# Order of the matmul passes within one weight tile: all with the high part first, then all with the low part

## The chip, the cores and the metric

The kernel runs on one core of a Trainium2 chip. The metric is the device time of one execution in microseconds (us). Before the change the median of three timed runs is 1946.19 us (1943.83 to 1947.27). One further execution was profiled; it took 1940.68 us.

## The reference, cut to what matters

One layer of a network on 256 tokens of width 2048: a mixer (gated delta rule, gated linear attention and a state-space part, merged by gates), cross attention to 256 memory tokens, and a convolved feed-forward block of hidden width 5632. All weights are float32. What matters for this change is that nearly all of the work is plain products of the 256 tokens with weight matrices:

```python
z = h @ w_in                          # 2048 x 14368, split into q, k, v, gates, ...
y_a = o_a @ w_dn_out                  # and w_gla_out, w_s5_glu, w_mix_out
q = h @ w_xa_q; kv = mem_n @ w_xa_kv  # and w_xa_out
gate, up = jnp.split(h @ w_ffn_up, 2, axis=-1)
y = (jax.nn.gelu(causal_depthwise_conv(gate, ffn_conv_w)) * up) @ w_ffn_down
```

## The kernel before

**Split numbers.** Each float32 operand is written as a high part in the type fp32r plus a low part (the remainder, also fp32r). A product is then three passes on TensorE: weight high by input high, weight high by input low, weight low by input high.

**Weight tiles.** Weights come in tiles of 2 blocks of 128 rows (KG = 2, the index kk) by 512 columns. `load_w` makes one: SyncE starts the DMA into `raw` (4 buffers), ScalarE casts it to `whi` (3 buffers, line 206, named CAST in the profile), and VectorE subtracts to get `wlo` (3 buffers, also line 206, TENSOR_TENSOR). A new `whi` can be cast when TensorE has read the oldest one for the last time; the same holds for `wlo`.

**Two forms of product.** `proj` gives a result with features on partitions: a weight block of 128x128 is the stationary operand, and the input moves. Its high pass (line 218; line 221 at the end of the contraction) streams 512 columns, which are the input's high and low halves side by side, and its low pass (line 219) streams 256. A tile has 4 output blocks m, so 8 high and 8 low passes. Before the change they alternate: for each m, for each kk, high then low. `proj_tok` gives tokens on partitions: 128 tokens of the input are stationary and 512 weight columns move. For each of two token halves t and each kk it makes the passes of lines 285 (weight high, input high), 286 (weight high, input low) and 287 (weight low, input high). `proj2` is `proj` over two weights at once, for the start of the feed-forward block. Results gather in PSUM tiles `acc`, of which there are five; those of `proj` are emptied by `total` (lines 225 and 226) and what follows it (in the delta-rule part `conv_silu`, lines 387 to 393).

**Order.** The engines run their own instructions in the order that the program lists, each waiting for what it needs. That order is fixed when the program is built: a scheduler that simulates a timeline picks from what is ready, with weight loads at a raised priority. So code order is only a start: it lets the scheduler move work of the background parts (the state-space recurrence of lines 932 to 934, the delta rule, the norms) and of the evacuations between the passes, and it also moves passes. A change in the passes can therefore move instructions of VectorE and ScalarE too, though the diff has none.

Of the kernel before, what the change touches and what calls it, by code (L numbers as in the profile page):

```python
# [9 lines left out]
F32 = mybir.dt.float32  # L10
# [8 lines left out]
P = 128  # L19
T = 256  # L20
# [3 lines left out]
NW = 512  # L24
KG = 2
# [11 lines left out]
N_ACC = 5  # L37
# [51 lines left out]
class Net:  # L89
# [116 lines left out]
            self.last = (nc.scalar.copy(hi, raw), self.seq(lambda: nc.vector.tensor_sub(lo, raw, hi.bitcast(F32))))  # L206
        return hi, lo

    def mm3(self, acc, hi, lo, x, start, stop):
        nc = self.nc  # L210
        if acc.shape[1] == T:
            nc.tensor.matmul(acc, hi, x[:, 0, :], start=start, stop=False)
            nc.tensor.matmul(acc, hi, x[:, 1, :], start=False, stop=False)
            nc.tensor.matmul(acc, lo, x[:, 0, :], start=False, stop=stop)
            return
        both = x.rearrange("p c s -> p (c s)")
        if not stop:
            nc.tensor.matmul(acc, hi, both, start=start, stop=False)  # L218
        nc.tensor.matmul(acc[:, :T], lo, x[:, 0, :], start=False, stop=False)  # L219
        if stop:  # L220
            nc.tensor.matmul(acc, hi, both, start=start, stop=True)  # L221

    def total(self, acc, out=None):
        r = self.row() if out is None else out
        self.nc.scalar.copy(r, acc[:, T:2 * T])  # L225
        self.nc.vector.tensor_add(r, r, acc[:, 0:T])  # L226
        return r

    def proj(self, w, KT, rhs, evac, n=NW, wide=True):
        nc = self.nc  # L230
        nm = (n + P - 1) // P
        accs = []
        for m in range(nm):
            a = self.ps_acc.tile([P, 512], F32, name="acc", tag="acc")
            accs.append(a[:min(P, n - m * P), :2 * T if wide else T])
        G = KT // KG
        for g in range(G):
            hi, lo = self.load_w(w, g, n)
            for m in range(nm):
                ms = slice(m * P, min(n, (m + 1) * P))  # L240
                for kk in range(KG):
                    kt = g * KG + kk
                    self.mm3(accs[m], hi[:, kk, ms], lo[:, kk, ms], rhs(kt), kt == 0, kt == KT - 1)
            if g < G - 1:
                self.pump()
        for m in range(nm):
            evac(m, accs[m])
        self.pump()

    def proj2(self, ws, KT, rhs, evac):  # L250
        nc = self.nc
        accs = []
        for i in range(6):
            a = self.ps_acc.tile([P, 512], F32, name="acc", tag="acc") if i < N_ACC else self.mx([P, 512])
            accs.append(a)
        for g in range(KT // KG):
            for i, w in enumerate(ws):
                nm = 4 - 2 * i
                hi, lo = self.load_w(w, g, nm * P)
                for m in range(nm):  # L260
                    ms = slice(m * P, (m + 1) * P)
                    for kk in range(KG):
                        kt = g * KG + kk
                        self.mm3(accs[4 * i + m], hi[:, kk, ms], lo[:, kk, ms], rhs(kt), kt == 0, kt == KT - 1)
                self.pump()
        for i in range(6):
            evac(i, accs[i])

    def proj_tok(self, w, KT, lhs, evac, n=NW, tail=1, mid=None):
        nc = self.nc  # L270
        accs = [self.ps_acc.tile([P, 512], F32, name="acc", tag="acc")[:, :n] for _ in range(2)]
        G = KT // KG
        wts = {}
        last = []

        def part(t, g):
            if g not in wts:
                wts[g] = self.load_w(w, g, n)
            hi, lo = wts[g]
            ts_ = slice(t * P, (t + 1) * P)  # L280
            for kk in range(KG):
                kt = g * KG + kk
                x = lhs(kt)
                xh, xl = (x[0], x[1]) if isinstance(x, tuple) else (x[:, 0, :], x[:, 1, :])
                nc.tensor.matmul(accs[t], xh[:, ts_], hi[:, kk, :], start=(kt == 0), stop=False)  # L285
                nc.tensor.matmul(accs[t], xl[:, ts_], hi[:, kk, :], start=False, stop=False)  # L286
                last[:] = [nc.tensor.matmul(accs[t], xh[:, ts_], lo[:, kk, :], start=False, stop=(kt == KT - 1))]  # L287

        for g in range(G - tail):
            for t in range(2):  # L290
                part(t, g)
            if mid and g == (G - tail) // 2:
                mid()
            self.pump()
        for t in range(2):
            with self.after(last if t and tail > 1 else ()):
                for g in range(G - tail, G):
                    part(t, g)
            evac(t, accs[t])
        self.pump()  # L300

# [1272 lines left out]
```

## Time and profile before

| what | value |
|---|---|
| median of three timed runs | 1946.19 us |
| profiled execution, time | 1940.68 us |
| profiled execution, span from first to last instruction | 1938.9 us |
| ScalarE (ACT) busy | 951.8 us, 49% |
| mean share of the 16 DMA engines, main queue | 54.9% |
| read from HBM | 350.47 MB, 187 GB/s over the span |

The profile names TensorE PE (its weight loads PEld), VectorE DVE, ScalarE ACT, GpSimd POOL and SyncE SP. A matmul's row gives its start and its duration, but matmuls are pipelined: the next one starts before the last has ended. So what a matmul costs is read from start to start, which is called its step here. In rows that merge several, the duration is from the first start to the last end.

### The profile page before, as it was taken

Reading aid. Unit: us, or ns where it says so; the run is one execution under the profiler, and the core shown is the slowest. Engines: PE = TensorE matmul, PEld = TensorE weight load, DVE = VectorE, ACT = ScalarE, POOL = GpSimd, SP = SyncE. Lnnn points to the kernel's source line nnn. Section 1 sums busy time; section 2 is a strip of 40 time slices with the busy share of each in tenths; the row PEclk is TensorE's granted clock in tenths of the full one; section 3 lists DMA queues with packets and bytes.
Section 4 is the critical chain, followed back from the end, with each engine's and each line's share of the span. In section 5 each row is a group of like instructions: output and inputs, shape, how many; then the busy total and the mean of one; then the engine's idle time right before and its main releaser. Section 6 shows DMA issues by size and latency. Waiting matters only on the chain.

```text
span 1938.9 us, 28177 instructions
## 1 busy us (share of the span) xinstructions
PE 1878.7 (97%) x10440; PEld 1565.4 (81%) x10440; DVE 1419.8 (73%) x2719; ACT 951.8 (49%) x1426; POOL 67.4 (3%) x117
## 2 busy tenths in 40 slices
PE   7989899999999999999999997999999999999997
PEld 6778788777778688878877986888888888888886
DVE  6878999996579999967666756766666666644445
ACT  5655544343565444444455655555555555534442
POOL 0000012020000000000000000000000000000000
PEclk9999999999999999999999998999999999999999
DMA  7535477684445576666576544655666555676664
GB/s 254 174 109 172 152 206 233 191 254 131 131 121 172 184 219 179 213 218 203 186 264 210 173 155 144 213 184 174 190 195 189 187 185 185 206 224 200 200 192 135
DMA packets 107482, 363.93 MB, mean 188 GB/s; under 512 B 12320, under 2 KB 20896, under 8 KB 106832
## 3 DMA queue, kind: packets, MB, share of 16 engines
q1 hardware_dynamic: 97696, 328.32, 54.9%
q0 software_dynamic: 9648, 33.81, 5.3%
q8 instruction: 82, 1.34, 0.3%
q14 instruction: 56, 0.46, 0.1%
HBM read 350.47 MB, written 11.61 MB: 187 GB/s over the span
## 4 chain that ended last, share of the span: by engine, by line
PE 86%; DVE 6%; issue 4%; DMA 2%; ACT 1%; POOL 0%; SPq 0%; DVEq 0%; ACTq 0%; POOLq 0%
PE acc L218 25%; PE acc L219 14%; PE acc L287 13%; PE acc L285 13%; PE acc L286 13%; DVE wlo L206 2%; PE acc L221 2%; PE mx L922 2%; DMA raw<-in 1%; DVE f L519 1%; DVE mm L932 0%; PE mx L183 0%; PE mx L947 0%; PE mx L641 0%; ACT whi L206 0%
## 5 line engine op out<-in xcount | busy, mean ns | idle before, releaser
L206 DVE TENSOR_TENSOR wlo<-raw,whi 128x1024 fp32r<-128x1024 f32 (+1 forms) x632 | 753.0, 1195 | 417.2 <-ACT whi L206 415.1
L206 ACT CAST whi<-raw 128x1024 fp32r<-128x1024 f32 (+1 forms) x632 | 646.7, 1029 | 724.8 <-PE acc L286 376.0
L218 PE MATMUL acc<-aa,whi 128*128 128x512 f32 x2085 | 725.8, 401 | 11.5 <-DVE r L226 9.7
L219 PE MATMUL acc<-aa,wlo 128*128 128x256 f32 x2224 | 555.2, 284 | 9.9 <-DVE wlo L206 9.9
L219 PEld LDWEIGHTS acc<-aa,wlo 128*128 128x128 f32 x2224 | 421.9, 190 | 53.3 <-DVE wlo L206 20.9
L218 PEld LDWEIGHTS acc<-aa,whi 128*128 128x128 f32 x2085 | 386.1, 190 | 82.2 <-issue 11.7
L285 PE MATMUL acc<-whi,aa 128*128 128x512 f32 (+1 forms) x704 | 269.8, 384 | 0.0
L286 PE MATMUL acc<-whi,aa 128*128 128x512 f32 (+1 forms) x704 | 268.4, 382 | 0.0
L287 PE MATMUL acc<-wlo,aa 128*128 128x512 f32 (+1 forms) x704 | 253.3, 385 | 3.7 <-DVE wlo L206 3.7
L287 PEld LDWEIGHTS acc<-wlo,aa 128*128 128x128 f32 x704 | 131.9, 188 | 33.6 <-DVE wlo L206 7.3
L286 PEld LDWEIGHTS acc<-whi,aa 128*128 128x128 f32 x704 | 132.4, 188 | 26.4 <-issue 1.1
L285 PEld LDWEIGHTS acc<-whi,aa 128*128 128x128 f32 x704 | 132.3, 188 | 26.2 <-issue 1.2
L285 PE MATMUL acc<-whi,ach 128*128 128x512 f32 x352 | 136.9, 389 | 0.0
L286 PE MATMUL acc<-whi,acl 128*128 128x512 f32 x352 | 136.9, 389 | 0.0
L287 PE MATMUL acc<-wlo,ach 128*128 128x512 f32 x352 | 123.4, 389 | 0.0
L932 DVE TENSOR_TENSOR mm<-M,X 128x128 f32<-128x128 f32 x254 | 98.6, 388 | 5.3 <-ACT X L926 0.6
L286 PEld LDWEIGHTS acc<-whi,acl 128*128 128x128 f32 x352 | 66.0, 188 | 13.8
L287 PEld LDWEIGHTS acc<-wlo,ach 128*128 128x128 f32 x352 | 66.1, 188 | 13.7
L285 PEld LDWEIGHTS acc<-whi,ach 128*128 128x128 f32 x352 | 66.1, 188 | 13.7
L934 DVE TENSOR_TENSOR X<-X,s__868 128x64 f32<-128x64 f32 x255 | 71.5, 280 | 4.5
L933 DVE TENSOR_TENSOR s__868<-mm 128x64 f32<-128x64 f32 x255 | 56.5, 222 | 4.7
L226 DVE TENSOR_TENSOR r<-r,acc 128x256 f32<-128x256 f32 x143 | 57.1, 414 | 0.4 <-ACT r L225 0.3
(454 smaller groups left out, 1865.6 us busy)
## 6 DMA issues: line engine op xcount, KB each, us to landing
raw<-in SPq DMA_DIRECT2D x600, 512.0 KB, 4.1
raw<-in SPq DMA_DIRECT2D x32, 256.0 KB, 2.7
gd<-r POOLq DMA_DIRECT2D x24, 256.0 KB, 4.7
f<-gd POOLq DMA_DIRECT2D x12, 512.0 KB, 5.3
f<-Rd POOLq DMA_DIRECT2D x4, 512.0 KB, 7.0
f<-in POOLq DMA_DIRECT2D x4, 512.0 KB, 4.0
gp<-in POOLq DMA_DIRECT2D x8, 256.0 KB, 4.5
xn<-in POOLq DMA_DIRECT2D x1, 2048.0 KB, 11.1
```

The source lines that it names most:

```text
L206: self.last = (nc.scalar.copy(hi, raw), self.seq(lambda: nc.vector.tensor_sub(lo, raw, hi.bitcast(F32))))
L218: nc.tensor.matmul(acc, hi, both, start=start, stop=False)
L219: nc.tensor.matmul(acc[:, :T], lo, x[:, 0, :], start=False, stop=False)
L221: nc.tensor.matmul(acc, hi, both, start=start, stop=True)
L226: self.nc.vector.tensor_add(r, r, acc[:, 0:T])
L285: nc.tensor.matmul(accs[t], xh[:, ts_], hi[:, kk, :], start=(kt == 0), stop=False)
L286: nc.tensor.matmul(accs[t], xl[:, ts_], hi[:, kk, :], start=False, stop=False)
L287: last[:] = [nc.tensor.matmul(accs[t], xh[:, ts_], lo[:, kk, :], start=False, stop=(kt == KT - 1))]
L922: nc.tensor.matmul(ps[:, n, c, :], self.Bl[c][rs, ft, :], su[rs, ft, tk], start=True, stop=True, tile_position=(32 * q, 0))
L932: nc.vector.tensor_mul(m, self.M, prev[:, None].broadcast_to([P, 2, 2, 32]))
L933: nc.vector.tensor_add(s, m[:, :, 0, :], m[:, :, 1, :])
L934: nc.vector.tensor_add(X[:, :, :, t], X[:, :, :, t], s)
```

## The change

Within one weight tile, `proj`, `proj2` and `proj_tok` now write all passes with `whi` first and all passes with `wlo` after them. In the last tile of a contraction, `proj` keeps the passes of one output block together (high, low, low, high), as before. The number, the shapes and the operands of the passes stay the same; so do the loads and all other code. A branch for 256-wide accumulators that nothing called is dropped.

```diff
-    def mm3(self, acc, hi, lo, x, start, stop):
-        nc = self.nc
...
-        both = x.rearrange("p c s -> p (c s)")
-        if not stop:
-            nc.tensor.matmul(acc, hi, both, start=start, stop=False)
-        nc.tensor.matmul(acc[:, :T], lo, x[:, 0, :], start=False, stop=False)
-        if stop:
-            nc.tensor.matmul(acc, hi, both, start=start, stop=True)
...
+    def tile_passes(self, accs, hi, lo, rhs, g, KT, n):
+        nc = self.nc
+        ks = [g * KG + kk for kk in range(KG)]
+        xs = [rhs(k) for k in ks]
+        ms = [slice(m * P, min(n, (m + 1) * P)) for m in range(len(accs))]
+
+        def high(m, kk):
+            nc.tensor.matmul(accs[m], hi[:, kk, ms[m]], xs[kk].rearrange("p c s -> p (c s)"), start=ks[kk] == 0,
+                             stop=ks[kk] == KT - 1)
+
+        def low(m, kk):
+            nc.tensor.matmul(accs[m][:, :T], lo[:, kk, ms[m]], xs[kk][:, 0, :], start=False, stop=False)
+
+        if ks[-1] < KT - 1:
+            for f in (high, low):
+                for m in range(len(accs)):
+                    for kk in range(KG):
+                        f(m, kk)
+            return
+        for m in range(len(accs)):
+            for kk in range(KG - 1):
+                high(m, kk)
+            for kk in range(KG):
+                low(m, kk)
+            high(m, KG - 1)
...
     def proj2(self, ws, KT, rhs, evac):
...
                 hi, lo = self.load_w(w, g, nm * P)
-                for m in range(nm):
-                    ms = slice(m * P, (m + 1) * P)
-                    for kk in range(KG):
-                        kt = g * KG + kk
-                        self.mm3(accs[4 * i + m], hi[:, kk, ms], lo[:, kk, ms], rhs(kt), kt == 0, kt == KT - 1)
+                self.tile_passes(accs[4 * i:4 * i + nm], hi, lo, rhs, g, KT, nm * P)
                 self.pump()
...
-        def part(t, g):
+        def passes(ts, g):
             if g not in wts:
                 wts[g] = self.load_w(w, g, n)
             hi, lo = wts[g]
-            ts_ = slice(t * P, (t + 1) * P)
-            for kk in range(KG):
-                kt = g * KG + kk
...
-                nc.tensor.matmul(accs[t], xh[:, ts_], hi[:, kk, :], start=(kt == 0), stop=False)
-                nc.tensor.matmul(accs[t], xl[:, ts_], hi[:, kk, :], start=False, stop=False)
-                last[:] = [nc.tensor.matmul(accs[t], xh[:, ts_], lo[:, kk, :], start=False, stop=(kt == KT - 1))]
...
+            for t in ts:
+                for kk in range(KG):
+                    for i in range(2):
+                        nc.tensor.matmul(accs[t], xs[kk][i][:, t * P:(t + 1) * P], hi[:, kk, :],
+                                         start=ks[kk] == 0 and i == 0, stop=False)
+            for t in ts:
+                for kk in range(KG):
+                    last[:] = [nc.tensor.matmul(accs[t], xs[kk][0][:, t * P:(t + 1) * P], lo[:, kk, :], start=False,
+                                                stop=ks[kk] == KT - 1)]
 
         for g in range(G - tail):
-            for t in range(2):
-                part(t, g)
+            passes(range(2), g)
```

In the changed kernel line 222 is the high pass of `proj` and line 226 its low pass, line 282 the two high passes of `proj_tok` and line 286 its low pass; `total` has moved to lines 211 and 212, and the lines behind `proj_tok` have moved up by one.

What the built programs list shows what the scheduler made of it. **First place: TensorE, the first weight tiles of the program** (`xset` is the split input, `acc` the accumulators). Before:

```order
L218 MATMUL acc<-xset,whi 128x512
L219 MATMUL acc<-xset,wlo 128x256
L218 MATMUL acc<-xset,whi 128x512
L219 MATMUL acc<-xset,wlo 128x256
L218 MATMUL acc<-xset,whi 128x512
L219 MATMUL acc<-xset,wlo 128x256
```

The same place in the changed program:

```order
L222 MATMUL acc<-xset,whi 128x512 x8
L226 MATMUL acc<-xset,wlo 128x256 x8
L222 MATMUL acc<-xset,whi 128x512 x8
L226 MATMUL acc<-xset,wlo 128x256 x8
L222 MATMUL acc<-xset,whi 128x512 x8
```

High and low passes have moved apart into runs of eight. At other places the scheduler keeps runs of two, where accumulators come free one by one. Counted over the whole list of TensorE, a low pass of `proj` follows directly on a high pass 1886 times before and 597 times now.

**Second place: VectorE, the end of the first slab of delta-rule keys** (`r1` and `f16` belong to `conv_silu` of the accumulators 840 and 841; `zs` is a copy for the state-space part; 1158 and 1180 are weight tiles of the next slab). Before:

```order
L206 TENSOR_TENSOR wlo_1158<-raw_1156,whi_1157 128x1024
L226 TENSOR_TENSOR r1_1054<-r1_1054,acc_840 128x256
L881 COPY zs_820<-mx_818 64x128
L206 TENSOR_TENSOR wlo_1180<-raw_1178,whi_1179 128x1024
L389 SCALAR_TENSOR_TENSOR r1_1057<-r1_1054,cwh_101,r1_1057 128x255
L389 SCALAR_TENSOR_TENSOR r1_1057<-r1_1054,cwh_101,r1_1057 128x254
L389 SCALAR_TENSOR_TENSOR r1_1057<-r1_1054,cwh_101,r1_1057 128x253
L393 SCALAR_TENSOR_TENSOR f16_837<-r1_1062,r1_1057 128x4x64
L226 TENSOR_TENSOR r1_1065<-r1_1065,acc_841 128x256
```

And in the changed program:

```order
L212 TENSOR_TENSOR r1_1054<-r1_1054,acc_840 128x256
L388 SCALAR_TENSOR_TENSOR r1_1057<-r1_1054,cwh_101,r1_1057 128x255
L388 SCALAR_TENSOR_TENSOR r1_1057<-r1_1054,cwh_101,r1_1057 128x254
L388 SCALAR_TENSOR_TENSOR r1_1057<-r1_1054,cwh_101,r1_1057 128x253
L206 TENSOR_TENSOR wlo_1180<-raw_1178,whi_1179 128x1024
L880 COPY zs_820<-mx_818 64x128
L392 SCALAR_TENSOR_TENSOR f16_837<-r1_1062,r1_1057 128x4x64
L212 TENSOR_TENSOR r1_1065<-r1_1065,acc_841 128x256
```

The three steps of the convolution for accumulator 840 have moved ahead of the low part 1180 and of the copy.

**Third place: VectorE, a few instructions later**, where the state-space part scales its input matrices (`f4_829`, `f4_830`, `bl`) from a table that a DMA brings. Before:

```order
L226 TENSOR_TENSOR r1_1086<-r1_1086,acc_842 128x256
L893 TENSOR_TENSOR f4_829<-f8_824,bl1_450 128x1024
L895 TENSOR_TENSOR f4_830<-f8_824,bl0_449 128x1024
L389 SCALAR_TENSOR_TENSOR r1_1089<-r1_1086,cwh_101,r1_1089 128x255
L900 TENSOR_TENSOR bl1_450<-f8_824,bl1_450 128x1024
L206 TENSOR_TENSOR wlo_1208<-raw_1206,whi_1207 128x1024
```

And in the changed program:

```order
L212 TENSOR_TENSOR r1_1086<-r1_1086,acc_842 128x256
L388 SCALAR_TENSOR_TENSOR r1_1089<-r1_1086,cwh_101,r1_1089 128x255
L388 SCALAR_TENSOR_TENSOR r1_1089<-r1_1086,cwh_101,r1_1089 128x254
L388 SCALAR_TENSOR_TENSOR r1_1089<-r1_1086,cwh_101,r1_1089 128x253
L206 TENSOR_TENSOR wlo_1208<-raw_1206,whi_1207 128x1024
L206 TENSOR_TENSOR wlo_1236<-raw_1234,whi_1235 128x1024
L206 TENSOR_TENSOR wlo_1264<-raw_1262,whi_1263 128x1024
L392 SCALAR_TENSOR_TENSOR f16_837<-r1_1094,r1_1089 128x4x64
L212 TENSOR_TENSOR r1_1097<-r1_1097,acc_843 128x256
L892 TENSOR_TENSOR f4_829<-f8_824,bl1_450 128x1024
```

Three low parts of weights have moved ahead of the first scaling instruction, which waits for the DMA. The list of SyncE is the same in both programs, instruction for instruction.

More of the change, by code (lines that the diff above doesn't have):

```diff
@@ L207, in load_w @@
         return hi, lo
-    def mm3(self, acc, hi, lo, x, start, stop):
-        nc = self.nc
[L211 to L215, printed above, removed]
-        both = x.rearrange("p c s -> p (c s)")
-        if not stop:
-            nc.tensor.matmul(acc, hi, both, start=start, stop=False)
-        nc.tensor.matmul(acc[:, :T], lo, x[:, 0, :], start=False, stop=False)
-        if stop:
-            nc.tensor.matmul(acc, hi, both, start=start, stop=True)
     def total(self, acc, out=None):
@@ L227, in total, with proj @@
         return r
-    def proj(self, w, KT, rhs, evac, n=NW, wide=True):
+    def tile_passes(self, accs, hi, lo, rhs, g, KT, n):
         nc = self.nc
-        nm = (n + P - 1) // P
-        accs = []
-        for m in range(nm):
-            a = self.ps_acc.tile([P, 512], F32, name="acc", tag="acc")
-            accs.append(a[:min(P, n - m * P), :2 * T if wide else T])
+        ks = [g * KG + kk for kk in range(KG)]
[18 more added lines that the diff above has]
+            high(m, KG - 1)
+    def proj(self, w, KT, rhs, evac, n=NW):
+        accs = [self.ps_acc.tile([P, 512], F32, name="acc", tag="acc")[:min(P, n - m * P)]
+                for m in range((n + P - 1) // P)]
         G = KT // KG
@@ L238, in proj @@
             hi, lo = self.load_w(w, g, n)
-            for m in range(nm):
-                ms = slice(m * P, min(n, (m + 1) * P))
-                for kk in range(KG):
-                    kt = g * KG + kk
-                    self.mm3(accs[m], hi[:, kk, ms], lo[:, kk, ms], rhs(kt), kt == 0, kt == KT - 1)
+            self.tile_passes(accs, hi, lo, rhs, g, KT, n)
             if g < G - 1:
                 self.pump()
-        for m in range(nm):
-            evac(m, accs[m])
+        for m, acc in enumerate(accs):
+            evac(m, acc)
         self.pump()
     def proj2(self, ws, KT, rhs, evac):
[L251 to L255, printed above, removed]
+        accs = [self.ps_acc.tile([P, 512], F32, name="acc", tag="acc") if i < N_ACC else self.mx([P, 512])
+                for i in range(6)]
         for g in range(KT // KG):
@@ L259, in proj2 @@
                 hi, lo = self.load_w(w, g, nm * P)
-                for m in range(nm):
-                    ms = slice(m * P, (m + 1) * P)
-                    for kk in range(KG):
-                        kt = g * KG + kk
-                        self.mm3(accs[4 * i + m], hi[:, kk, ms], lo[:, kk, ms], rhs(kt), kt == 0, kt == KT - 1)
+                self.tile_passes(accs[4 * i:4 * i + nm], hi, lo, rhs, g, KT, nm * P)
                 self.pump()
@@ L279, in part @@
             hi, lo = wts[g]
-            ts_ = slice(t * P, (t + 1) * P)
[L281 to L287, printed above, removed]
+            ks = [g * KG + kk for kk in range(KG)]
+            xs = [(x[0], x[1]) if isinstance(x, tuple) else (x[:, 0, :], x[:, 1, :]) for x in map(lhs, ks)]
+            for t in ts:
[7 more added lines that the diff above has]
+                                                stop=ks[kk] == KT - 1)]
         for g in range(G - tail):
-            for t in range(2):
-                part(t, g)
+            passes(range(2), g)
             if mid and g == (G - tail) // 2:
@@ L297, in proj_tok @@
                 for g in range(G - tail, G):
-                    part(t, g)
+                    passes([t], g)
             evac(t, accs[t])
```

## The prediction

> **What bounds the kernel now.** I read the page first: span, busy shares, the chain that ended last.
>
> ```profile
> span 1938.9 us, 28177 instructions
> PE 1878.7 (97%) x10440; PEld 1565.4 (81%) x10440; DVE 1419.8 (73%) x2719; ACT 951.8 (49%) x1426; POOL 67.4 (3%) x117
> PE 86%; DVE 6%; issue 4%; DMA 2%; ACT 1%; POOL 0%; SPq 0%; DVEq 0%; ACTq 0%; POOLq 0%
> ```
>
> TensorE is busy for 97% of the span and makes 86% of the chain. So two things can gain: a shorter step from pass to pass, or a shorter wait of TensorE. Second, the view of waits of PE.
>
> ```profile
> PE acc L219 <- DVE wlo L206: 10.6, 7, 4.3
> ...
> PE acc L218 <- DVE r L226: 9.7, 8, 2.2
> ...
> PE acc L287 <- DVE wlo L206: 4.0, 7, 1.3
> ```
>
> Waits for a low part are 10.6 + 4.0 = 14.6 us; that is all that "low passes later" can aim at directly. Waits for an accumulator (L226) are 9.7. Third, busy time by stage; the columns are the window, its length, then busy time and count of PE, PEld, DVE, ACT and POOL, the granted clock, the DMA share and GB/s.
>
> ```profile
> 60.00:112.00 52.00, 42.53 (x232) 35.74 (x231) 42.41 (x117) 25.63 (x39) 3.20 (x5) 0.97 0.57 170
> 180.00:240.00 60.00, 54.77 (x309) 47.12 (x308) 57.90 (x159) 28.84 (x45) 0.00 (x0) 0.97 0.50 154
> 360.00:400.00 40.00, 36.28 (x154) 28.12 (x153) 39.93 (x53) 14.79 (x15) 2.40 (x5) 1.00 0.65 195
> 1170.00:1230.00 60.00, 49.91 (x268) 41.92 (x268) 40.89 (x91) 33.98 (x70) 3.43 (x5) 0.91 0.49 158
> 1230.00:1700.00 470.00, 470.00 (x2640) 404.06 (x2640) 323.74 (x506) 242.31 (x377) 1.27 (x2) 1.00 0.61 193
> ```
>
> The long feed-forward stretch (1230 to 1700) has no idle TensorE at all; there only the step counts. The waits sit in four short stretches. In two of them (180:240, 360:400) VectorE itself is full, so a wait removed there only moves.
>
> **Term 1, the step.** The number of passes stays. What changes is which pass follows which. Alternating passes of `proj` (view: timeline of PE):
>
> ```profile
> 601.30 0.39 PE L218 MATMUL acc<-aa,whi 128*128 128x512 f32 x1
> 601.53 0.28 PE L219 MATMUL acc<-aa,wlo 128*128 128x256 f32 x1
> ...
> 603.42 0.40 PE L218 MATMUL acc<-aa,whi 128*128 128x512 f32 x1
> ```
>
> From 601.30 to 603.42 there are six pairs: 0.353 us a pair. For passes in a run, one run of four high passes, a stretch of 512-wide passes of `proj_tok`, and its 256-wide passes:
>
> ```profile
> 1604.90 1.08 PE L218 MATMUL acc<-aa,whi 128*128 128x512 f32 x4
> ```
>
> ```profile
> 999.75 0.39 PE L285 MATMUL acc<-whi,mgx 128*128 128x512 f32 x1
> ...
> 1002.47 0.39 PE L285 MATMUL acc<-whi,mgx 128*128 128x512 f32 x1
> ```
>
> ```profile
> 1128.42 0.28 PE L286 MATMUL acc<-whi,aa 128*128 128x256 f32 x1
> ...
> 1130.33 0.28 PE L287 MATMUL acc<-wlo,aa 128*128 128x256 f32 x1
> ```
>
> High in a run: (1.08 - 0.39)/3 = 0.230, or 2.72/12 = 0.227 in the second piece. A 256-wide pass in a run: 1.91/16 = 0.119. A pair in runs is then 0.346 to 0.349 against 0.353: 4 to 7 ns less, for each border of high to low that goes. Of these, 1886 - 597 = 1289 go, so 5 to 9 us. I take the row of the same line (0.230), 5 us, and of it 3.5, since some three tenths of the `proj` tiles (the first eight of 38 slabs and the start of the feed-forward block among them) lie in stretches where TensorE waits anyway. `proj_tok` passes are all of one width there (0.227 whichever follows), so they gain nothing in step. Bounds: 0 and -9 us.
>
> **Term 2, an evacuation that comes earlier.** TensorE starts the second key slab when accumulators come free:
>
> ```profile
> 94.24 1.28 ACT L392 ACT_TABLE_LOAD   x1 [2.36 <-DVE r L389]
> 96.89 0.47 PE L218 MATMUL acc<-aa,whi 128*128 128x512 f32 x1 [2.18 <-DVE r L226]
> ```
>
> ScalarE sat 2.36 us for L389, because VectorE did the low part 1180 first; in the new order L389 stands ahead of it (second place of the change). The release of accumulator 841 then comes up to 2.4 us sooner, and the 2.18 us wait mostly goes. What is late next is accumulator 842; its wait, another of the eight in the view of waits, stays. I take -2 (0 to -2.2). In this part ScalarE also gets two more table loads, 1.28 us each by the row above. They stand ahead of a cast behind which ScalarE idled:
>
> ```profile
> 84.78 1.05 ACT L206 CAST whi<-raw 128x1024 fp32r<-128x1024 f32 x1 [1.73 <-PE acc L218]
> ```
>
> 1.73 of the 2.56 us is covered there; the remaining 0.8 comes off ScalarE's lead, which may be as long as three `whi` buffers allow (a tile is 8 x 0.353 = 2.8 us of TensorE). I cost it at nothing, and 0.8 if that lead is gone.
>
> **Term 3, the longest wait for a low part.**
>
> ```profile
> 102.47 1.08 PE L218 MATMUL acc<-aa,whi 128*128 128x512 f32 x4
> 102.81 1.23 DVE L893 TENSOR_TENSOR f<-f,bl 128x1024 f32<-128x1024 f32 x1 [2.67 <-DMA f<-zd]
> ...
> 106.62 2.35 DVE L206 TENSOR_TENSOR wlo<-raw,whi 128x1024 fp32r<-128x1024 f32 x2
> ...
> 107.90 0.39 PE L219 MATMUL acc<-aa,wlo 128*128 128x256 f32 x1 [4.35 <-DVE wlo L206]
> ...
> 108.93 0.63 PE L219 MATMUL acc<-aa,wlo 128*128 128x256 f32 x2
> ```
>
> VectorE idled 2.67 us for a DMA, then ran four instructions of the state-space part and the convolution, then the low part (1208) on which TensorE hung for 4.35 us. After so long a wait the matmuls ran slower for a while (the last row: two low passes in 0.63); the granted clock of 0.97 in 60:112 is 1.6 us of lost clock, of which I put 1.2 here. Now 1208 stands ahead of the DMA-bound instruction (third place), and eight high passes, not four, cover it: 0.9 us more of cover. The displaced VectorE work follows between later low parts, where a tile takes TensorE 2.8 us and VectorE 1.2. I take -5 (0 to -5.6).
>
> **Term 4, transposes behind a convolution.** A wait of 2.06 us stands before the transposes of one value head:
>
> ```profile
> 223.44 0.66 PE L398 MATMUL mx<-cst,f 128*128 128x128 f32 x4 [2.06 <-DVE f L393]
> ```
>
> In the new list 12 instead of 4 passes of `proj_tok` stand between the last tile and them: 8 x 0.227 = 1.8 us of cover. VectorE is full in this stretch (57.90 of 60), so I take -1 (0 to -2.1).
>
> **Term 5, low parts where VectorE is full.** Most of the 4.0 us of L287 waits lie in 360:400, where TensorE idles 3.7 us and VectorE is busy 39.93 of 40. Four more high passes ahead (0.9 us) shift TensorE's need once, not at each tile: -1 (+1 to -4).
>
> **Term 6, the start of the feed-forward block.** Here the longest of the other waits for a low part stand, as:
>
> ```profile
> 1199.64 0.39 PE L219 MATMUL acc<-aa,wlo 128*128 128x256 f32 x1 [2.44 <-DVE wlo L206]
> ```
>
> Six more high passes now stand ahead of such a low pass, but four of them also stand ahead of the transposes that feed VectorE's queue in front of that low part; both sides shift by about 1.3 us. 0 (+1.5 to -4).
>
> **Term 7, a new wait near 485 us.** In ScalarE's list one `whi` cast (tile 4889) has moved behind five instructions of the state-space output, and its low part on VectorE behind some fifteen.
>
> ```profile
> 492.07 0.63 ACT L956 ACTIVATE f<-f 128x512 f32<-128x512 f32 x1 [2.04 <-DVE f L953]
> 492.61 0.57 ACT L926 COPY X<-mx 128x512 f32<-128x512 f32 x1
> ```
>
> Three of the one and two of the other are 3.0 us; the passes moved ahead of it on TensorE cover about two. Behind the waiting high pass stand all later passes, so this is on the path: +1 (0 to +4).
>
> Sum: -3.5 - 2 - 5 - 1 - 1 + 0 + 1 = -11.5 us. It is made on the profiled time, 1940.68, giving 1929.2; that execution was 5.5 us under the median of the runs, so against the median it is 1946.19 - 11.5 = 1934.7, say 1935. About 0.2%, 3.9 us, is what can be told from no change here.
>
> **A weight load's price.** A rule that could speak against the change is the time of a load, since each low pass of 0.119 us has to hide one:
>
> ```profile
> L219 PEld LDWEIGHTS acc<-aa,wlo 128*128 128x128 f32 x2224 | 421.9, 190 | 53.3 <-DVE wlo L206 20.9
> ```
>
> The row says 190 ns a load. The Trainium skill, page "TensorE: Matmul & The Clock Gate", section "LDWEIGHTS (loading the stationary operand)", gives columns / 1.2 GHz, an estimate of 107 ns for 128. By that the loads just fit under a low pass and the sum stays; the steps of 0.119 above agree with it rather than with 190, which is then a latency.
>
> **Rivals.** (a) *Weight loads bind in runs of low passes.* In the old order each low load had a 0.23 us high pass beside it. If the full 190 ns of the row showed in long runs, each of the 1289 passes would cost 71 ns more: +92 us, some 2030. The change ends slower by 0.2% when a low pass in a run steps above 0.131 (12 ns more x 1289 = 15.5, against the 11.5 gained). Against it: 16 steps of 0.119 in a row, in a run of loads alike. For it: that run was not of this line, and runs of low passes over two hardly occur before. 10%. (b) *VectorE takes it back.* From 180 us on it is full in two windows, so microseconds won at 100 could turn into longer waits at 200 and 380. Then only the step in the feed-forward stretch remains, 2 to 3 us: 1943, no change that can be told. Against it: what VectorE does there also waits for TensorE's slabs, and it idles before. 14%. (c) *The scheduler's new order costs elsewhere*, as at 485 us with its full 4 us, and term 3 brings only half: -11.5 + 3 + 2.5 = -6, and with one more such place -3: 1943. 8%.
>
> **The numbers.** Forecast 68%: 1935, its own range 1927 to 1942. With (b) and (c) at 1943 to 1946 the range that leaves out 2 in 10 is 1926 to 1946: the lower end has the step at its better bound with terms 2 to 5 near theirs, and (a) stays outside. Faster 0.68, same 0.22, slower 0.10.
>
> **What would show it.** Right: in the feed-forward stretch a tile of eight high and eight low passes takes 2.79 us instead of 2.82; the waits for L206 near 108 us and for an accumulator near 97 are gone; PE's low passes wait for `wlo` under 8 us in all. Wrong: steps of low passes above 0.13; a wait of several us near 485; longer waits for L226 (now line 212) at 190 to 225 that eat what came before.

## The result, and the profile after

The changed kernel takes **1926.19 us** (median of four runs, 1920.51 to 1927.01) where the kernel before took 1945.9 on the same chip; the ratio is 0.9896, 95% interval 0.9884 to 0.9908. It is 19.7 us faster, and 11.5 were forecast. In a later series four more runs of the changed kernel took 1919.94 to 1923.7; the median of all eight is 1922.9.

The profiled execution took 1925.81 us, 14.9 under the profiled one of before. That is less than the medians differ by, because the profiled execution of before was a quick one: 1940.68, with a mean granted clock of 0.993, where of 51 later runs of that kernel (1939.8 to 1949.6, clock mostly 0.990 or 0.991) two were as quick. A difference between two profiles that builds up before 1230 us is therefore uncertain by some microseconds: the three kernels below that are the old program up to there lie 2.0 to 4.6 us behind the profile of before at that point. From 1230 us to the last ten microseconds the clock is full in both.

The page after: span, busy time, the chain that ended last.

```profile
span 1924.0 us, 28133 instructions
PE 1873.0 (97%) x10440; PEld 1573.9 (82%) x10440; DVE 1415.4 (74%) x2719; ACT 959.6 (50%) x1428; POOL 67.4 (4%) x117
PE 89%; DVE 6%; ACT 2%; issue 1%; DMA 1%; DVEq 0%; SPq 0%; POOL 0%; ACTq 0%; POOLq 0%
```

TensorE is busy 5.7 us less with the same 10440 passes, the span is 14.9 us shorter, and the share of "issue" (time in which an engine waited for nothing that the profile shows) in the chain went from 4% to 1%. The waits of PE after (what, us in total, times, longest):

```profile
PE acc L222 <- DVE r L212: 8.3, 5, 2.5
PE acc L226 <- DVE wlo L206: 7.7, 8, 2.9
...
PE acc L286 <- DVE wlo L206: 2.7, 6, 0.8
```

Waits for a low part fell from 14.6 to 10.4 us, those for an accumulator from 9.7 to 8.3. The windows after, with the columns as before:

```profile
60.00:112.00 52.00, 48.03 (x268) 40.48 (x268) 43.65 (x121) 31.07 (x46) 3.20 (x5) 1.00 0.61 185
112.00:180.00 68.00, 65.34 (x380) 55.48 (x380) 49.50 (x123) 34.57 (x59) 0.00 (x0) 0.90 0.37 112
180.00:240.00 60.00, 56.90 (x332) 49.20 (x331) 57.54 (x154) 30.38 (x46) 0.00 (x0) 1.00 0.54 170
1230.00:1700.00 470.00, 470.00 (x2662) 411.29 (x2661) 322.82 (x500) 250.33 (x376) 1.27 (x2) 1.00 0.63 196
```

TensorE does 268 matmuls between 60 and 112 us where it did 232: the wait that term 3 aimed at is gone, and most of that of term 2. But from 112 to 180 the clock is 0.90, where it was 1.00 before:

```profile
112.00:180.00 68.00, 66.79 (x433) 57.30 (x433) 51.80 (x127) 39.60 (x66) 0.00 (x0) 1.00 0.45 138
```

I return to that. In the feed-forward stretch TensorE is full before and after, and yet does 22 matmuls more in the same 470 us.

To see where time is won, count the passes over weights on TensorE in order of time and compare when the k-th starts. "Idle" is the sum of the gaps on PE in which no matmul ran, up to there. The experiments in the table follow below.

| k-th pass | before, us | change | proj_tok only | early proj only | all but early proj | pairs | idle before / change / early only |
|---|---|---|---|---|---|---|---|
| 512 | 129.5 | -13.3 | +0.5 | -13.2 | +2.3 | -8.2 | 9.8 / 4.1 / 4.4 |
| 1024 | 242.5 | -1.0 | +0.1 | -2.6 | +2.2 | +1.0 | 16.3 / 9.9 / 9.9 |
| 1280 | 306.7 | -1.1 | +0.1 | -1.6 | +2.2 | +1.0 | 16.3 / 9.9 / 10.5 |
| 1792 | 429.1 | -2.1 | -0.8 | +6.2 | +0.7 | -0.7 | 20.0 / 12.6 / 15.3 |
| 2048 | 514.4 | -3.9 | -2.6 | +1.3 | -0.9 | -0.9 | 21.6 / 12.7 / 15.3 |
| 3328 | 832.1 | -2.4 | -1.4 | +1.3 | -0.2 | -0.3 | 24.8 / 17.6 / 18.4 |
| 3584 | 896.4 | -4.5 | -3.5 | +1.2 | -2.3 | -2.3 | 24.8 / 17.6 / 18.4 |
| 4352 | 1076.5 | -8.2 | -6.7 | +1.5 | -6.0 | -6.5 | 27.6 / 17.7 / 21.4 |
| 5120 | 1239.8 | -7.9 | -6.6 | +2.0 | -5.9 | -6.7 | 38.3 / 28.7 / 32.5 |
| 7680 | 1694.4 | -14.8 | -6.7 | +1.8 | -12.9 | -13.4 | 38.3 / 28.7 / 32.5 |

Two things stand out. Between passes 5120 and 7680, the feed-forward block, the change wins 6.9 us although no idle time goes. And the 13 us of lead at the 512th pass are not all saved time: 5.7 are idle time that went, but the new order also puts 64 small matmuls (56 of the state-space part, line 922 before, and 8 transposes, line 398) behind that point instead of ahead of it (79 matmuls that are no weight pass have run by then instead of 143), and they are still to be done.

### The profile page after: what moved, and what is told of

Read it like the earlier page. It is cut to its first block, busy times and chain, and to the rows that moved or that the text cites. A ratio compares the mean times of both kernels' runs of the same rounds, so it can differ in the third digit from the quotient of the medians.

```text
span 1924.0 us, 28133 instructions
## 1 busy us (share of the span) xinstructions
PE 1873.0 (97%) x10440; PEld 1573.9 (82%) x10440; DVE 1415.4 (74%) x2719; ACT 959.6 (50%) x1428; POOL 67.4 (4%) x117
## 4 chain that ended last, share of the span: by engine, by line
PE 89%; DVE 6%; ACT 2%; issue 1%; DMA 1%; DVEq 0%; SPq 0%; POOL 0%; ACTq 0%; POOLq 0%
PE acc L282 28%; PE acc L222 27%; PE acc L286 14%; PE acc L226 14%; DVE wlo L206 2%; PE mx L921 2%; DMA raw<-in 1%; ACT whi L206 1%; DVE r L388 1%; PE mx L183 0%; PE mx L640 0%; DVE mm L931 0%; DVE f L518 0%; PE mx L946 0%; DVE X L933 0%
## 5 line engine op out<-in xcount | busy, mean ns | idle before, releaser
L222 PE MATMUL acc<-aa,whi 128*128 128x512 f32 x2224 | 620.7, 398 | 10.7 <-DVE r L212 8.3
L226 PEld LDWEIGHTS acc<-aa,wlo 128*128 128x128 f32 x2224 | 345.4, 191 | 59.1 <-DVE wlo L206 11.5
L226 PE MATMUL acc<-aa,wlo 128*128 128x256 f32 x2224 | 362.1, 283 | 7.6 <-DVE wlo L206 7.4
L282 PE MATMUL acc<-whi,aa 128*128 128x512 f32 (+1 forms) x1408 | 346.5, 383 | 0.0
L282 PEld LDWEIGHTS acc<-whi,aa 128*128 128x128 f32 x1408 | 255.3, 188 | 53.3 <-issue 2.3
L286 PE MATMUL acc<-wlo,aa 128*128 128x512 f32 (+1 forms) x704 | 191.5, 383 | 2.8 <-DVE wlo L206 2.7
L286 PEld LDWEIGHTS acc<-wlo,aa 128*128 128x128 f32 x704 | 127.9, 188 | 31.5 <-DVE wlo L206 6.6
L286 PE MATMUL acc<-wlo,ach 128*128 128x512 f32 x352 | 95.4, 389 | 0.0
L282 PEld LDWEIGHTS acc<-whi,ach 128*128 128x128 f32 x352 | 66.1, 188 | 13.7
L286 PEld LDWEIGHTS acc<-wlo,ach 128*128 128x128 f32 x352 | 66.1, 188 | 13.7
L282 PEld LDWEIGHTS acc<-whi,acl 128*128 128x128 f32 x352 | 66.0, 188 | 13.7
L282 PE MATMUL acc<-whi,mgx 128*128 128x512 f32 x256 | 64.3, 391 | 0.1
L211 ACT COPY r<-acc 128x256 f32<-128x256 f32 x143 | 49.6, 362 | 27.3 <-PE acc L222 26.8
```

The lines of the kernel that those rows point to most:

```text
L222: nc.tensor.matmul(accs[m], hi[:, kk, ms[m]], xs[kk].rearrange("p c s -> p (c s)"), start=ks[kk] == 0, stop=ks[kk] == KT - 1)
L226: nc.tensor.matmul(accs[m][:, :T], lo[:, kk, ms[m]], xs[kk][:, 0, :], start=False, stop=False)
L282: nc.tensor.matmul(accs[t], xs[kk][i][:, t * P:(t + 1) * P], hi[:, kk, :], start=ks[kk] == 0 and i == 0, stop=False)
L286: last[:] = [nc.tensor.matmul(accs[t], xs[kk][0][:, t * P:(t + 1) * P], lo[:, kk, :], start=False, stop=ks[kk] == KT - 1)]
```

## The experiments

All compute the full result. Each ratio is to the runs of the kernel before in the same session.

**Only the feed-forward slabs in the new order.** Three kernels; the first groups whole slabs of the feed-forward block, the second only each slab's first weight tile, the third all tiles but the first.

```diff
-            for m in range(nm):
+            if self.grouped:             # second: and g == 0; third: and g > 0
+                self.tile_passes(accs, hi, lo, rhs, g, KT, n)
+            else:
...
+    n.grouped = True                     # ahead of the feed-forward slabs
     for s in range(22):
```

> The old kernel with the new order in the 21 feed-forward slabs of proj alone; everything up to about 1230 us is the old program, instruction for instruction. Theory step (the change shortens the path by what a pass costs after one of its own kind, and by a small wait at each slab start that goes): this stretch alone gains 7 us, 0.36 us a slab, and the total is 1938 to 1940 against 1946, ratio 0.996 to 0.997. Rival (the gain of the feed-forward stretch comes from the earlier stages, which leave buffers and queues in another state): under 2 us, ratio above 0.999.

> The old kernel with the new order in the first weight tile of each feed-forward slab only (7 of 8 tiles keep alternating). If the gain there is the small wait of about 0.2 us for a low part at each slab start, as the old trace has it, this gains most of that: 3 to 4 us in all, 0.16 to 0.2 a slab. If the gain is the step alone, one tile of eight gains 0.03 us a slab, 0.6 us in all, which cannot be told from none.

> The complement: the new order in all tiles of a feed-forward slab but the first. Step alone: six tiles (the last one is not changed) of about 0.03 us, 0.17 us a slab, 3.5 us in all, and the small waits at the slab start stay. If the waits carry the gain: under 1 us.

Measured: 1938.96 us (0.9972, 0.9962 to 0.9982), 1942.39 (0.9993, 0.9983 to 1.0003) and 1938.88 (0.9972, 0.9962 to 0.9981), against 1944.59. The median of the second cannot be told from before; its trace can. From pass 5120 to 7680 the three win 7.0, 2.7 and 5.7 us. The 7.0 is the whole of what the change wins there, and it is 0.35 us for each of 20 slabs. The first tile is one of eight but brings 2.7 us, and the two parts together would make 8.4, so they overlap, and neither is what the step alone (0.6 and 3.5) or the waits alone (3 to 4, and under 1) were to give: something other than the step is paid once a slab. The view of waits of PE shows nothing there. That of the weight loads does; before, between 1230 and 1700 us:

```profile
PEld acc L219 <- DVE wlo L206: 7.8, 20, 0.4
```

Twenty waits, one for each slab. One of them in the timeline of the matmuls, before:

```profile
1264.72 0.28 PE L219 MATMUL acc<-aa,wlo 128*128 128x256 f32 x1
1264.84 1.08 PE L218 MATMUL acc<-aa,whi 128*128 128x512 f32 x4
1265.91 0.39 PE L219 MATMUL acc<-aa,wlo 128*128 128x256 f32 x1
1266.13 0.39 PE L218 MATMUL acc<-aa,whi 128*128 128x512 f32 x1
```

and the load of that low pass:

```profile
1265.91 0.19 PEld L219 LDWEIGHTS acc<-aa,wlo 128*128 128x128 f32 x1 [0.43 <-DVE wlo L206]
```

The four high passes at the slab's start take 1.07 us from start to start, where the run rate of 0.230 makes 0.92, and the low pass behind them steps 0.22 instead of 0.117. The lateness is hidden from the view of PE because a pass's modelled end (0.39 behind its start) covers it. Over 18 slabs of the stretch, what these two steps have above the median of their kind is 3.8 us, 0.21 a slab, so by this estimate 4.2 us for twenty. The other 2.8 of the 7.0 us is the step proper, 2.2 ns for each of 1280 pairs. In the changed kernel the view has no such wait there any more, in the first and third of these one of 0.4 at most; in the second, which keeps the rest of the slab in the old order, 6.1 us of it stay:

```profile
PEld acc L220 <- DVE wlo L207: 6.1, 21, 0.3
```

**Only `proj_tok` in the new order.** The kernel before, with the changed kernel's `proj_tok`.

```diff
         for g in range(G - tail):
-            for t in range(2):
-                part(t, g)
+            passes(range(2), g)
```

> The old kernel with the new order in proj_tok alone. Its passes are all equally wide, so theory step expects nothing from steps. Theory slack (low parts needed later, high parts free earlier) expects the waits for a cast near 1010 and 1023 us (2.5 us, with what follows 3.6) to go, and some of the low part waits at 360 to 400 (4.0): -3 to -8 us. Theory step alone: within 1 us of the old kernel.

Measured: 1935.67 us (0.9952, 0.9931 to 0.9973), 8.9 under before and just beyond the 3 to 8 expected: nearly half of the whole gain, from passes to which the prediction gave next to nothing. The table shows where it comes in: up to pass 2048, from 3328 to 4352, and not at all in the feed-forward block. At two places the trace shows what changed. First, before, two casts near 1010 and 1023 us held TensorE up (weight loads, 1000 to 1060 us):

```profile
PEld acc L285 <- ACT whi L206: 3.4, 2, 1.8
```

The first of these casts stands in ScalarE's list behind an instruction that waits for a DMA (`mch`); with `proj_tok` only it stands ahead of it. ScalarE before, then `proj_tok` only:

```profile
1007.43 1.71 ACT L308 ACTIVATE aa<-mch,vec 128x256 fp32r<-128x256 f32 x4 [4.98 <-DMA mch<-in]
1009.04 1.03 ACT L206 CAST whi<-raw 128x1024 fp32r<-128x1024 f32 x1
```

```profile
998.97 1.05 ACT L206 CAST whi<-raw 128x1024 fp32r<-128x1024 f32 x1 [0.49 <-PE acc L285]
1004.04 1.71 ACT L310 ACTIVATE aa<-mch,vec 128x256 fp32r<-128x256 f32 x4 [4.02 <-DMA mch<-in]
```

So it was its place in the list that held this cast up, and not TensorE's last reading of an older `whi`. Two kernels below confirm it: in `proj` only, with the old `proj_tok`, the cast stands behind a DMA wait of 4.84 us again and TensorE waits for it; with the low part first, where `whi` is read until a tile's last pass, the cast stands ahead (1017.78, the DMA wait ends at 1021.30) and TensorE does not wait. 1.0 us of such waits is left here, at the second place, 0.5 in the change; why the second one is shorter is not shown. In the same window 1.2 us of waits for a low part went altogether. Second, from 830 to 900 us small products of the state-space output (L947 before, L949 here) stand between the passes. Each time TensorE turns to them, the load of the first shows some 0.35 us of "issue". Before, and then `proj_tok` only:

```profile
PEld mx L947 <- issue: 2.1, 6, 0.4
```

```profile
PEld mx L949 <- issue: 0.7, 2, 0.4
```

In the new list they stand together (one row has 64 of them), so TensorE turns to them twice instead of six times. That is 1.4 us, and at 0.20 for each return to the wide passes another 0.8: 2.2, against the 2.1 us won from pass 3328 to 3584. The scheduler did that; the diff doesn't say it.

**Only `proj` in the new order**, `proj_tok` as before.

> proj grouped as in the change, proj_tok left in its old order. If what the two halves bring adds up: the change's profile was 14.9 us under before, proj_tok alone 6.7, so proj alone is 8 us under before, median 1936 to 1938, of which 7 in the feed-forward slabs (k = 5120 to 7680 of the weight passes) and about 1 before the first proj_tok. The program up to 180 us is the change's, so the half clock after 119 us should be there again. Rival (the halves need each other: proj_tok's gain only shows once proj no longer waits): over 10 us under before, 1931 to 1935.

Measured: 1934.99 us (0.9937, 0.9925 to 0.995), 12.3 under before; 7.0 of it in the feed-forward passes, as expected. The time is under the 1936 to 1938 expected and lies in the rival's range. With `proj_tok` alone the two add up to 21.2 us, and the change itself was 25.9 under before in this series of runs and 19.7 in the first. The series differ by more than the question needs, so these medians do not tell whether the halves add up or need each other.

**The low part first.**

```diff
-            for f in (high, low):
+            for f in (high, low) if g == 0 else (low, high):
```

and the same in `proj_tok`.

> Each tile (but a slab's first and last) passes with the low part first, then all with the high part: as few borders of high to low as in the change, but the low part is needed before its eight high passes instead of behind them, and whi comes free later instead of earlier. Theory (the gain is the step in the feed-forward stretch, plus slack for VectorE's low part and ScalarE's next cast elsewhere): the feed-forward stretch keeps 4 to 7 of its 7 us, the rest is lost or turns: waits of PE for wlo rise above 15 us in all, the casts wait for whi again near 1010 and 1023, time 1936 to 1950. Rival (only the number of borders counts): 1925 to 1930, waits as in the change.

Measured: **1969.85 us** (1.0114, 1.0101 to 1.0128), slower than both and beyond the 1936 to 1950 expected. The passes stand in runs as in the change, and low passes in a run step 0.120 as there, so runs alone do not make the gain. Each slab now waits in the open (groups by line, 1230 to 1700 us, then one wait in the timeline of PE):

```profile
L226 PE MATMUL acc<-aa,wlo 128*128 128x256 f32 x1285 | 203.8, 283 | 14.6 <-DVE wlo L206 14.6
```

```profile
1399.68 1.22 PE L226 MATMUL acc<-aa,wlo 128*128 128x256 f32 x8 [0.77 <-DVE wlo L206]
1400.74 2.00 PE L222 MATMUL acc<-aa,whi 128*128 128x512 f32 x8
```

From pass 5120 to 7680 this kernel takes 14.5 us longer than before and 21.4 longer than the change. 14.6 of these are open gaps, about 0.7 at a slab; most of the rest is lateness that the modelled ends cover, as above: two steps at each slab have, with the gaps, 20.4 us above the median of their kind. Why it is once a slab, VectorE and then ScalarE show:

```profile
1397.03 0.42 DVE L1449 TENSOR_TENSOR r<-r,rfr 128x256 f32<-128x256 f32 x1
1398.40 1.23 DVE L206 TENSOR_TENSOR wlo<-raw,whi 128x1024 fp32r<-128x1024 f32 x1 [0.95 <-ACT whi L206]
```

```profile
1397.31 1.05 ACT L206 CAST whi<-raw 128x1024 fp32r<-128x1024 f32 x1 [1.22 <-PE acc L222]
```

After the evacuation of the slab before, VectorE waits for the cast, and the cast waited until TensorE had read `whi` of an earlier tile for the last time, which in this order is the tile's very last pass. Of my expectation, the feed-forward stretch did not keep part of its gain but lost 14.5 us, and TensorE does not wait again for the casts near 1010 and 1023, since here too the cast stands ahead of the DMA wait.

**The state-space core one slab later**, and the changed kernel again, in the same series.

```diff
-    if not SP5:
-        s5 = n.spawn(n.s5_core(s5_cr, s5_ci), R_S5)
     section("dk", 1, n.dn_k)
+    if not SP5:
+        s5 = n.spawn(n.s5_core(s5_cr, s5_ci), R_S5)
```

> The change, with the state-space core begun one slab later (behind the first key slab). Theory: the 13 us of half clock from 120 to 134 us come from 24 small matmuls (L921, 32 rows each) right behind two short waits; begun where TensorE has run long without a wait, the clock stays at 1.00, and of the 6.8 us lost there 4 to 7 come back: 1919 to 1923. Rival 1: the cluster lowers the clock wherever it stands; half clock some 30 us later, 1925 to 1928. Rival 2: the clock stays full, but VectorE is full from 180 us on and takes it back: first passes near 162 us 5 to 7 us earlier than in the change, near 242 us no longer so, 1925 to 1928.

> The changed kernel itself, unaltered. If the half clock after 119 us belongs to this program, its profile has it again (granted clock 0.90 in 112 to 180 us, mean 0.990 or 0.991) and the time is 1925 to 1927; the one run at mean clock 0.993 took 1920.5, so runs without it should be 5 to 7 us shorter.

Measured: 1926.52 us (0.9899, 0.9883 to 0.9914) and 1921.4 (0.9868, 0.9854 to 0.9881), the second under the 1925 to 1927 expected. These were to explain the granted clock of 0.90. In the changed kernel's first profile three slices of 4 us (windows, the clock is the third number from the end):

```profile
122.00:126.00 4.00, 4.00 (x15) 3.15 (x14) 1.47 (x4) 1.79 (x5) 0.00 (x0) 0.50 0.31 116
126.00:130.00 4.00, 4.00 (x16) 3.36 (x15) 2.18 (x5) 0.81 (x3) 0.00 (x0) 0.50 0.00 0
130.00:134.00 4.00, 4.00 (x15) 3.53 (x15) 2.28 (x13) 2.75 (x6) 0.00 (x0) 0.50 0.00 0
```

My theory laid that on 24 small matmuls that stand there. It falls: the same kernel in its second profile has a full clock at that place, and the dip comes later and is shorter:

```profile
124.00:128.00 4.00, 4.00 (x28) 3.44 (x27) 3.03 (x9) 2.96 (x8) 0.00 (x0) 1.00 0.00 0
...
136.00:140.00 4.00, 4.00 (x20) 3.20 (x18) 2.37 (x3) 1.78 (x5) 0.00 (x0) 0.67 0.78 217
140.00:150.00 10.00, 10.00 (x55) 8.46 (x54) 4.85 (x18) 4.33 (x6) 0.00 (x0) 0.84 0.35 124
```

With the core moved, the half clock was there from 124 to 136 us all the same, neither gone nor 30 us later. So the dip comes in each profile of these three, at a place that moves, and costs 3.4 us (granted clock 0.95 in the 68 us from 112 to 180) to 6.8 (0.90); what sets it off stays open.

It does not belong to the change alone. By the clock records of the traces, each of the thirteen profiles has 3.4 to 13.7 us of half clock between 97 and 151 us; before has 3.4 from 108.7 on. Up to pass 1024 the clock cost (half of the time at half clock) 6.8 us in the first profile of the change, 5.1 with early `proj` only, 3.4 with `proj` only, 3.4 in the second profile of the change, and 3.4 before. These four lead before at that pass by 1.0, 2.6, 4.3 and 4.0 us, so what they differ by there is the clock.

**Only the eight early slabs of `proj`, and all but these.** One flag turns the new order of `proj` off, or on, at the first gates (about 190 us); the first kernel has the old `proj_tok`, the second the new one.

```diff
+    n.grouped = False                    # early only; all but early: False ahead, True here
     gates(0, G1)
```

> Only the eight proj slabs before the first gates (up to about 190 us) are grouped; all else in the old order. Theory (terms 2 to 4 are real and are partly handed on): TensorE's idle time up to the 512th weight pass falls from 9.8 to 4 us as in the change, and 3 to 6 us of it reach the end: 1939 to 1943. Rival (VectorE, full from 180 us on, or a lowered clock takes all of it back): within 2 us of before, and the waits for a low part in proj_tok between 240 and 430 us longer than before's.

> The change everywhere but in those eight proj slabs, which keep the old order. If what the early slabs bring reaches the end, this is 3 to 6 us over the change (1923 over its eight runs so far): 1926 to 1929. Rival (it is taken back by the end): 1921 to 1924. The wait of 4 us for a low part near 104 to 108 us is there again either way.

Measured: 1942.05 us (0.9984, 0.9973 to 0.9996), 3.0 under before, and 1928.87 (0.9914, 0.9898 to 0.993), 16.2 under before, where the change was 19.7 and 25.9 in its two series. Both are as expected. So the early slabs are worth 3 us alone, and within the whole 3.5 to 9.7, as the series differ. The table shows what becomes of it alone: the 5.4 us less idle time at pass 512 is still there at 5120 (32.5 against 38.3). But from pass 1280 to 2048 a lead of 1.6 us turns into a lag of 1.3, in the stretch where VectorE is full (the 6.2 at pass 1792 is in part order, since 48 more small matmuls have run there by then). `proj` only goes the same way, from a lead of 2.9 to a lag of 2.4. The change, `proj_tok` only and all but early `proj` win 2.7 to 3.1 us in that stretch, and the three kernels with the old program there moved by -0.3 to +2.2. The waits of the weight loads of `proj_tok` for a low part, 300 to 440 us, before, early `proj` only, and the change:

```profile
PEld acc L287 <- DVE wlo L206: 7.3, 9, 1.7
```

```profile
PEld acc L313 <- DVE wlo L207: 12.0, 20, 1.5
```

```profile
PEld acc L286 <- DVE wlo L206: 6.6, 10, 1.2
```

With the old order in `proj_tok` (line 313 there) these waits rise by 4.7 us (to 11.8 with `proj` only), so rival (b) fits this part by itself. With the new order in both they don't rise.

**Runs of two.**

```diff
-            for f in (high, low):
-                for m in range(len(accs)):
+            for m in range(len(accs)):
+                for f in (high, low):
                     for kk in range(KG):
```

> proj in runs of two (two high, two low, for each of the four row blocks) instead of eight; proj_tok as in the change. Four borders of high to low a tile instead of one in the change. In the change's runs the first two high passes step 234 ns and only the third to eighth 227 to 231, so by the theory (run length, and slack for the low part) the feed-forward stretch keeps 0 to 3 of its 7 us, the early waits for a low part are back, and the time is 1931 to 1938. Rival (each border costs the same): 4/7 of the gain in the feed-forward stretch, 4 us, and 1926 to 1930.

Measured: 1931.44 us (0.9928, 0.9912 to 0.9944). Between passes 5120 and 7680 it wins 6.7 us, nearly all of the change's 6.9, where I had expected 0 to 3 and the rival 4: both are wrong. The time lies in the expected 1931 to 1938, but not for the expected reason. Its passes there (timeline of PE):

```profile
1604.37 0.63 PE L222 MATMUL acc<-aa,whi 128*128 128x512 f32 x2
1604.84 0.40 PE L226 MATMUL acc<-aa,wlo 128*128 128x256 f32 x2
1605.08 0.62 PE L222 MATMUL acc<-aa,whi 128*128 128x512 f32 x2
```

Two high and two low take 0.70 to 0.71 us, 0.349 a pair (mean step of this stretch, doubled), against 0.3486 in the change and 0.354 before with its late low passes, 0.351 without them. The lists are mixed: the scheduler made runs of eight of about a quarter of the low passes here, and it had left the change itself in twos for part of each slab. But groups of two and two taken by themselves step 0.349 a pair in both kernels, and so do groups of eight and eight. So it is enough that passes come in twos. What the pairs lack is ahead: idle time up to pass 1024 is 17.0 us, as before (16.3), where the change has 9.9.

No kernel here was faster than the change.

## Why the prediction was wrong in size

The direction held; the sum was too small. The 1926.19 lies 0.8 us under the forecast's own range (1927 to 1942) and at the edge of the wider one (from 1926), and the 1922.9 of all eight runs lies under both.

**Term 1, and "there only the step counts": the step that failed.** I read "no idle TensorE at all" from the busy time of PE, took the feed-forward stretch for two to three microseconds of step and its start for nothing. The start is that (term 6: from pass 4608 to 5120 the change takes 0.5 us more). The stretch itself brought 7.0 us. The step proper was even smaller than forecast (2.2 ns a pair, not 4 to 7): the 0.353 of an alternating pair came from one piece at 601 us, and this stretch has 0.351 without its late passes. But 4.2 us came from a wait in each of twenty slabs that the busy time of PE hides and the waits of the weight loads show. The 7.0 us are shown by grouping these slabs alone, and the wait by the loads' 7.8 us that are gone; the split into 4.2 and 2.8 is worked out from the steps. The low part first shows the other side: a low part that comes late is paid once a slab there too (+14.5).

**Term 1 on `proj_tok`, "so they gain nothing in step".** That is right: 0.227 us in both kernels. In time they won 8.9 us by themselves, where terms 4, 5 and 7 gave them -1 in all. Term 4: the wait before the transposes went from 2.06 to 0.97 us, as forecast (last row below), but by luck. With `proj_tok` alone in the new order it is still 2.08, and with only the early slabs of `proj` it is 0.99; no pass of `proj_tok` runs before 237 us in these traces, so they cannot cover it. What about the early slabs shortens it is not shown. Term 5: from pass 1280 to 1792 the change took 1.0 us less, as forecast. Term 7 had the wrong sign: waits of PE for `whi` come to 0.2 us in the whole kernel, and from pass 1792 to 2048 (429 to 514 us) the change was 1.8 us faster. Not foreseen at all were the casts near 1010 and 1023 us and the state-space products that stand together from 830 to 900. From pass 3328 to 4352, where they stand, lie 5.3 us of the 6.7 in the table's column; the other 1.4, and what lies between 6.7 and the 8.9 of the medians, I have not put to a cause.

**Terms 2 and 3** removed what they named. The timeline at these places after:

```profile
96.50 0.70 PE L222 MATMUL acc<-aa,whi 128*128 128x512 f32 x2 [0.80 <-DVE r L212]
...
104.86 2.00 PE L222 MATMUL acc<-aa,whi 128*128 128x512 f32 x8
106.70 1.11 PE L226 MATMUL acc<-aa,wlo 128*128 128x256 f32 x8
...
223.17 0.66 PE L397 MATMUL mx<-cst,f 128*128 128x128 f32 x4 [0.97 <-DVE f L392]
```

The 2.18 us wait is 0.80, the 4.35 us wait is gone, and idle time up to pass 512 is 5.7 us less, where I had 2 and 3.8. The lists carry it: in the kernel with runs of two, where the low parts stand behind the DMA-bound instruction again, both waits are back with 2.32 and 2.87 us. The clock was wrong: I counted 1.2 us as won because no long wait was left to lower it. Up to pass 1024 it costs 3.4 us before and 3.4 or 6.8 in the two profiles of the change. So of the 8 us of terms 2 to 4, about 4 are left at pass 1024 where the clock costs as much as before, and 3 reach the end alone.

**The remaining slabs of `proj`** (between the first gates and the feed-forward block) should carry what is left, 12.3 - 5.6 - 3.0 = 3.7 us. That is a difference of three medians, each known to about 2 us, so it cannot be told from nothing; no kernel isolated them.

**The rivals.** (a) is out: in the changed kernel low passes in runs of eight step 0.120, with 191 ns a load in the groups by line. (b) fits the early slabs alone, but not the change, where with `proj_tok`'s own new order the waits for a low part do not rise (7.3 and 6.6 us). (c) did not come; at the two places that were followed, the casts and the state-space products, the scheduler's new order was a gain.

The forecast tile of 2.79 us is met (1278.91 - 1276.13 = 2.78):

```profile
1276.13 1.99 PE L222 MATMUL acc<-aa,whi 128*128 128x512 f32 x8
1277.95 1.11 PE L226 MATMUL acc<-aa,wlo 128*128 128x256 f32 x8
1278.91 2.00 PE L222 MATMUL acc<-aa,whi 128*128 128x512 f32 x8
```

## What to carry to other kernels

A matmul engine that shows 100% busy can still be kept waiting: a wait shorter than a matmul's modelled duration appears only in the waits of its weight loads, so read these, and count them against the loop (twenty waits, twenty slabs). When passes are put in another order, ask for each operand buffer how much later it is needed; in the feed-forward stretch that slack was worth more than the step (4.2 against 2.8 us). And look in the new lists for work that has moved ahead of an instruction that waits for a DMA: that is what took away the 4.35 us wait of term 3 and the cast's wait near 1010 us, though the diff has nothing of it.

## What the hardware showed that I had not expected

The granted clock fell to 0.50 for some 13 us while TensorE was busy. Ahead of it stand two short gaps (changed kernel, timeline of PE):

```profile
118.03 0.51 PE L226 MATMUL acc<-aa,wlo 128*128 128x256 f32 x2 [0.65 <-DVE wlo L206]
118.37 0.63 PE L222 MATMUL acc<-aa,whi 128*128 128x512 f32 x2
119.17 3.11 PE L921 MATMUL mx<-f,bl 32*128 32x128 f32 x24 [0.16 <-DVE bl L897]
```

The Trainium skill, page "TensorE: Matmul & The Clock Gate", section "Part 1: The HAM clock gate (the "warmup" mystery)", knows two rates, half and full, set by windows of about 3.4 us of activity. The slices of 0.50 and 1.00 agree with two rates, and the matmuls go with them (15 or 16 in 4 us against 28); the stretches of half clock before 1230 us in the thirteen traces last 3.4 us or two, three or four times that. A half clock of several such windows at full busy time does not follow from that, and here the measurement decides. The same program had the dip 17 us later, and shorter, in another execution.

In the feed-forward stretch of the change a 512-wide high pass steps on average 227 ns from the sixth of a run on, but 233 to 234 as the first and second behind low passes; a low pass right behind a high one steps 116, further on in a run 119 to 120. What the border costs the one pass it gives back in part to the other, so long runs win little over pairs.
